# A second score product over 64 rows instead of 128, in an encoder layer with two attention head groups

## The chip, the cores and the metric

The kernel runs on one core of a Trainium2 chip. A core has a matrix engine (TensorE, "PE" in the profile, with its weight loads shown apart as "PEld"), three engines for elementwise work (VectorE "DVE", ScalarE "ACT", GpSimd "POOL"), and queues that issue DMA transfers; nearly all DMAs of this kernel are issued by SyncE ("SP"). The metric is the time in microseconds of one execution on the device, from outside; the profiled execution also has a span, from its first to its last instruction.

## What is computed

One layer on a sequence of 1024 rows of width 1024, in float32. An input projection feeds two groups of eight heads of width 64: attention with a forget gate (FoX, causal) and attention over a band of chunks with a relative-position bias. Both go through an output projection; a cross-attention into 256 memory rows and an MLP of width 4096 follow, each with a norm before and after it. Cut to the part that the change touches:

```python
logits = jnp.einsum('bqhd,bkhd->bhqk', qb, kb).astype(jnp.float32) * scale      # FoX, blocks of 128 queries
logits = logits + c[:, :, q0:q1, None] - c[:, :, None, :q1]
...
logits = jnp.einsum('bcqhd,bckhd->bhcqk', qc, kband).astype(jnp.float32) * scale  # chunked
logits = logits + bias[None, :, None]
...
p = jax.nn.softmax(logits, axis=-1).astype(v.dtype)
out = jnp.einsum('bhcqk,bckhd->bcqhd', p, vband)
```

## The kernel before

**Precision.** TensorE multiplies in a rounded format (`F32R`). To keep float32 accuracy, each operand is split into a hi part (rounded) and a lo part (the remainder), and a product is made of three: hi x hi, hi x lo and lo x hi (`mm3`, lines 191 to 195). A head is only 64 wide, while the array has 128 rows, and the scores use this. For head `a` of a pair, `HALVES[a]` (line 360) names its own 64 rows and the other 64. The tile `qs` holds the queries' hi part in the head's own rows and their lo part in the other rows (lines 837 to 844). The tile `kd` holds the keys' hi part twice, once in each half; the second time by a DMA from SBUF to SBUF. The tile `kl` holds the keys' lo part twice, in the same way. So the first product over 128 rows (line 638) gives q_hi k_hi + q_lo k_hi, and the second one (line 639), accumulated into the same bank of PSUM, gives q_hi k_lo + q_lo k_lo.

**Where the keys come from.** `project_steps` (line 792) makes the projections of a pair of heads. For keys, per half `th` of the 1024 rows and per head `a`: ScalarE copies the hi part into the head's own rows of `kd` (line 847), VectorE subtracts to get the lo part into the own rows of `kl` (line 848), and `copy` (line 849) sends each to the other 64 rows, 128 KB a transfer. Over 8 pairs, 2 halves and 2 heads that makes 32 transfers of `kd` and 32 of `kl`.

**What sets the order.** In the attention phase the order of instructions on every engine is written out while the kernel is built, by a planner (`Flow`, line 56). It keeps an estimated clock for each engine. Steps of TensorE come from generators (`value_steps`, `turn_steps`, `score_steps`, `side_steps`, then the projections as filler), each with a cost and a condition; work for the other engines is put into waiting lists with a due time, a cost and a priority. A DMA costs 0.55 us of the queue there, and lands after the time given. A block of keys and queries counts as ready (`seen["qk", n]`) when twelve parts have reported; `score_steps` (line 604) yields one step per score piece, of up to 512 columns, when its keys, its bias and a bank are there. So what is told to the planner decides in which order score pieces, transposes, value products and projections interleave.

**The score pieces.** A head has eight blocks of 128 queries and twelve pieces. Each piece is the two products at lines 638 and 639, then VectorE adds the bias and takes the minimum (the queries are negated; line 642), ScalarE exponentiates, GpSimd scales. Transposes (line 711) and the products with the values (line 754) follow.

**The start.** While the first loads are under way, TensorE does 17 transposes of the identity (line 1628) into a bank that nobody reads. The first real products are those of the values (lines 1681 and 193 to 195). The squares of the input for its norm (`square`, line 1633) use a ring of two buffers with the tag `phl`, which the attention phase uses later for the split probabilities.

Of the kernel before, what the change touches and what calls it, by code (L numbers as in the profile page):

```python
# [15 lines left out]
F32R = mybir.dt.float32r  # L16
# [6 lines left out]
P = 128  # L23
# [4 lines left out]
HT = 512  # L28
# [6 lines left out]
def f(ap):  # L35
    return ap.bitcast(F32)
# [99 lines left out]
def build(ctx, tc, nc, out, t):  # L136
    def pool(name, bufs=1, space=None, stack=ctx, **kw):
        if space is not None:
            kw["space"] = space
        return stack.enter_context(tc.tile_pool(name=name, bufs=bufs, reuse_waits="tile", **kw))  # L140
# [9 lines left out]
    def mm_tile(shape, name, tag="mm"):  # L150
        return psp.tile(shape, F32, tag=tag, bufs=2, name=name)
# [104 lines left out]
    p1 = pool("p1", stack=p1s)  # L256
# [103 lines left out]
    HALVES = [(slice(a * 64, a * 64 + 64), slice(64 - a * 64, 128 - a * 64)) for a in range(2)]  # L360
    flow = Flow()
# [8 lines left out]
    def mark(key):  # L370
        return lambda at: seen.__setitem__(key, at)
# [179 lines left out]
    bias, qs, kd, kl, vs2, probs, trs, pvs = {}, {}, {}, {}, {}, {}, {}, {}  # L551
# [40 lines left out]
    def block_range(kind, i):  # L592
        return 0 if kind == "f" else max(0, i - 4)
# [10 lines left out]
    def score_steps():  # L604
# [5 lines left out]
        for n, a in heads:  # L610
            kind, pr = ORDER[n]
            h = pr * 2 + a
            for g in groups(n):
                probs[n, a, g] = {}
                for q in (1, 0) if kind == "f" else (0, 1):
                    i = 2 * g + q
                    nm = f"{kind}{h}g{g}{i}"
                    b0 = block_range(kind, i)
                    nk = (i + 1 - b0) * P
                    k0, boff = b0 * P, 0 if kind == "f" else 640 - nk  # L620
                    first = nk if nk <= 512 else 512 if nk - 512 >= 256 else nk - 256
                    pieces = [(0, first), (first, nk - first)] if nk > first else [(0, nk)]
                    mn = small.tile([P, 2], F32, tag="mn", bufs=6, name=f"mn{nm}")
                    fresh = g > 1 or not probs[n, a, g]
                    for j, (o, w) in enumerate(pieces):
                        wide = w
                        last = j == len(pieces) - 1
                        yield (2 * (wide / 2400 + 0.0135),
                               lambda: there(("qk", n), ("bias", n, a)) and free["s"].ready()
                               and (not fresh or j or free["sp"].ready()))  # L630
                        free["s"].take()
                        if fresh and not j:
                            free["sp"].take()
                            tile_ = p1.tile([P, S], F32, tag="sp", bufs=5, name=f"sp{nm}")
                        sp = tile_ if g > 1 else tile_[:, q * HT:(q + 1) * HT]
                        ps = mm_tile([P, HT], f"s{nm}{j}", "s")
                        qb = qs[n, a][:, i * P:(i + 1) * P]
                        nc.tensor.matmul(ps[:, :wide], qb, kd[n, a][:, k0 + o:k0 + o + wide], start=True, stop=False)
                        nc.tensor.matmul(ps[:, :wide], qb, kl[n, a][:, k0 + o:k0 + o + wide], start=False, stop=True)

                        def reduce(o=o, w=w, j=j, ps=ps, sp=sp, mn=mn, bt=bias[n, a], boff=boff):
                            nc.vector.tensor_tensor_reduce(
                                out=sp[:, o:o + w], in0=ps[:, :w], in1=bt[:, boff + o:boff + o + w],
                                scale=1.0, scalar=3e38 if j == 0 else mn[:, 0:1],
                                op0=ALU.add, op1=ALU.min, accum_out=mn[:, j:j + 1])

                        if not last:
                            flow.put("V", flow.end, 0.15 + w / 950, reduce, free["s"].give)
                        else:
                            sm = small.tile([P, 2], F32, tag="sm", bufs=6, name=f"sm{nm}")  # L650
                            exp = lambda sp=sp[:, :nk], m=mn[:, j:j + 1], sm=sm: nc.scalar.activation(
                                sp, sp, AF.Exp, scale=-1.0, bias=m, accum_out=sm[:, 0:1])
                            inv = lambda sm=sm: nc.vector.reciprocal(sm[:, 1:2], sm[:, 0:1])
                            mul = lambda sp=sp[:, :nk], sm=sm: nc.gpsimd.tensor_scalar(
                                sp, sp, sm[:, 1:2], 1.0, op0=ALU.mult, op1=ALU.mult)
                            rest = [("S", 0.25 + nk / 1090, exp), ("V", 0.17, inv), ("G", 0.25 + nk / 1150, mul)]
                            end_of_head = i == (0 if kind == "f" else TB - 1)

                            def after(at, rest=rest, key=("p", n, a, g, q), end_of_head=end_of_head, kind=kind, i=i):
                                free["s"].give(at)  # L660
                                if kind == "f" and i:
                                    mask_block(*key[1:3], i - 1, at)
                                if end_of_head:
                                    free["bias"].give(at)
                                flow.chain(at, rest, mark(key), 0)

                            go = lambda at, w=w, reduce=reduce, after=after: flow.put("V", at, 0.15 + w / 950, reduce, after)
                            if kind == "f":
                                ready[n, a, i] = go
                                masked[n, a, i](flow.end)  # L670
                            else:
                                go(flow.end)
                            probs[n, a, g][q] = sp, b0, i
# [118 lines left out]
    def project_steps(what, n, part):  # L792
# [7 lines left out]
        for th in range(2):  # L800
            cs = slice(th * HT, (th + 1) * HT)
            for kc in range(KC):
                yield (0.681, lambda: kc or there((what, n)) and free["mm"].ready() and
                       (th or free["u4"].ready(u) and (what != "k" or free["klo"].ready(2))))
                if kc == 0:
# [7 lines left out]
                    ps = mm_tile([P, HT], f"{what}{n}_{th}")  # L813
# [17 lines left out]
            for a, (own, oth) in enumerate(HALVES):  # L831
                def last(at, both=both):
                    both.append(at)
                    if len(both) == 2:
                        free["mm"].give(at)

                if what == "q":
                    pv = ps.rearrange("p (a b) -> p a b", b=P)[:, :, ::1 if kind == "f" else -1]
                    dst = qs[n, a].rearrange("p (a b) -> p a b", b=P)[:, th * 4:th * 4 + 4, :]
                    hi = lambda dst=dst, pv=pv, own=own: nc.scalar.activation(dst[own], pv[own], AF.Copy, scale=-0.125)  # L840
                    lo = lambda dst=dst, pv=pv, own=own, oth=oth: nc.vector.scalar_tensor_tensor(
                        dst[oth], pv[own], -0.125, f(dst[own]), op0=ALU.mult, op1=ALU.subtract)
                    flow.put("S", flow.end, 0.6, hi, lambda at, lo=lo, last=last: flow.put(
                        "V", at, 0.7, lo, lambda end: (last(end), part(end)), 1), 1)
                else:
                    d, l = kd[n, a], kl[n, a]
                    hi = lambda d=d, ps=ps, own=own, cs=cs: nc.scalar.activation(d[own, cs], ps[own], AF.Copy)
                    lo = lambda d=d, l=l, ps=ps, own=own, cs=cs: nc.vector.tensor_sub(l[own, cs], ps[own], f(d[own, cs]))
                    copy = lambda x, own=own, oth=oth, cs=cs: nc.sync.dma_start(f(x[oth, cs]), f(x[own, cs]))

                    def then(at, lo=lo, last=last, copy=copy, d=d, l=l):
                        flow.load(at, lambda: copy(d), part, 2.3)
                        flow.put("V", at, 0.7, lo, lambda end: (last(end), flow.load(
                            end, lambda: copy(l), part, 2.3)), 1)

                    flow.put("S", flow.end, 0.6, hi, then, 1)
        free["w"].give(flow.end)
# [751 lines left out]
    with tc.manual_schedule():  # L1609
# [14 lines left out]
        raw0 = [value_raw(0, 0)]  # L1624
        vs = {g: value_tiles(g) for g in (1, 0)}
        warm = mm_tile([P, 4, P], "warm", "tr")
        for n in range(17):
            nc.tensor.transpose(warm[:, n % 4, :], ident, ident)

        sqs = [p1.tile([P, 2, HT], F32, tag="phl", bufs=2, name=f"sqx{j}") for j in range(2)]  # L1630
        sq = [sqs[0][:, 0]]
# [63 lines left out]
        ps = mm_tile([P, 4], "ssx", "pv")  # L1695
# [26 lines left out]
        for th in (1, 0):  # L1722
            tr = mm_tile([P, 4, P], f"rr{th}", "pv")
# [60 lines left out]
    o = [outs[1, h] for h in range(4)]  # L1784
# [206 lines left out]
    for b in range(4):  # L1991
        c = slice(b * P, (b + 1) * P)
        ps = mm_tile([P, HT], f"ym11{b}", "tr" if b < 2 else "pv")
# [36 lines left out]
    k0, k1 = slice(0, HT), slice(HT, D)  # L2030
# [141 lines left out]
    with manual:  # L2172
        sums = lambda: None
        for j in range(NP):
# [10 lines left out]
            if j < AHEAD:  # L2185
                p1, g11 = saved.pop(j)
# [210 lines left out]
        last = inverse_last(7)  # L2397
# [69 lines left out]
```

## Time and profile before

| what | us |
|---|---|
| median of two runs | 1461.92 (1461.62 and 1462.22) |
| span of the profiled execution | 1459.5 |
| VectorE busy in it | 996.0 |
| ScalarE busy in it | 820.7 |
| GpSimd busy in it | 421.0 |
| scores on TensorE, first and last product | about 87 to 472 |

The profile comes from one execution. An engine's busy time is the time covered by its instructions. Matmuls overlap, as they are pipelined, and their ends are modelled; the time that one of them takes of TensorE is better read from the distance between starts. A row of the timeline has the start, the duration, the engine, the line, the operation, the tiles (out, then in) and the shape; in brackets stands the idle time before it and what ended it. Rows in a row with the same line and tile are merged (x8, for instance). In the shape of a matmul, 128*128 is the active rows and columns of the array.

### The profile page before, as it was taken

How to read it: one execution, taken by the hardware profiler on the slowest of the kernel's cores; microseconds unless marked ns; L12 is line 12 of the kernel's file. 1: busy time of each engine (PE TensorE's matmuls, PEld its weight loads, DVE VectorE, ACT ScalarE, POOL GpSimd, SP SyncE). 2: the span in 40 equal slices, each digit the busy share in tenths (PEclk: the TensorE clock that was granted, in tenths of full speed). 3: DMA queues.
4: the chain of work that ended last, by engine and by line, in shares of the span. 5: the costliest groups of instructions: out<-in, count | busy, mean ns of one | idle time of the engine just before them, and what ended most of it. 6: DMA issues, size and time to landing. Idle time of an engine off the chain costs nothing.

```text
span 1459.5 us, 21037 instructions
## 1 busy us (share of the span) xinstructions
PE 1447.7 (99%) x7265; PEld 1222.2 (84%) x7265; DVE 996.0 (68%) x1704; ACT 820.7 (56%) x1437; POOL 421.0 (29%) x520
## 2 busy tenths in 40 slices
PE   9999999999999999999999999999999999999998
PEld 8988888888889888888788888888888888888886
DVE  6777777767668847976873687765555666655576
ACT  6567677766677836555653465545555543444442
POOL 1245456555455301521332414343322000000021
PEclk9999999999999999999999999999999999999999
DMA  7132324321325584552541637754444785445565
GB/s 276 49 95 72 83 67 140 86 82 46 95 58 161 174 314 173 187 179 86 181 138 44 200 132 260 258 196 159 159 151 161 286 318 185 140 149 190 186 246 202
DMA packets 88987, 232.17 MB, mean 159 GB/s; under 512 B 10649, under 2 KB 14753, under 8 KB 88881
## 3 DMA queue, kind: packets, MB, share of 16 engines
q1 hardware_dynamic: 88736, 230.57, 47.6%
q8 instruction: 57, 0.93, 0.3%
q14 instruction: 50, 0.40, 0.1%
q10 hardware_dynamic: 144, 0.26, 0.1%
HBM read 167.30 MB, written 55.11 MB: 152 GB/s over the span
## 4 chain that ended last, share of the span: by engine, by line
PE 96%; DVE 2%; DMA 1%; ACT 1%; issue 0%; SPq 0%; DVEq 0%; ACTq 0%
PE pv L754 4%; PE fx L194 4%; PE fx L193 4%; PE fx L195 4%; PE ptr L711 4%; PE px L194 3%; PE fy L193 3%; PE px L195 3%; PE fy L195 3%; PE px L193 3%; PE fy L194 3%; PE mq L195 2%; PE q L193 2%; PE q L195 2%; PE q L194 2%; PE yw L193 2%
## 5 line engine op out<-in xcount | busy, mean ns | idle before, releaser
L717 DVE TENSOR_TENSOR phl<-ptr,phl 128x512 fp32r<-128x512 f32 (+1 forms) x152 | 92.5, 616 | 31.5 <-ACT phl L720 30.5
L2163 ACT ACTIVATE whif<-ra 128x1024 fp32r<-128x1024 f32 x37 | 39.2, 1061 | 130.3 <-PE fy L194 62.6
L2165 DVE TENSOR_TENSOR wlof<-ra,whif 128x1024 fp32r<-128x1024 f32 x37 | 45.3, 1225 | 91.7 <-ACT whif L2163 91.7
L720 ACT ACTIVATE phl<-ptr 128x512 fp32r<-128x512 f32 (+1 forms) x152 | 79.8, 540 | 40.3 <-PE ptr L711 38.5
L2285 POOL TENSOR_SCALAR rf<-sf 128x1 f32<-128x1 f32 x7 | 7.9, 1130 | 321.7 <-ACT jf L2266 321.4
L754 PE MATMUL pv<-phl,vs 128*128 128x512 f32 (+1 forms) x304 | 85.2, 366 | 0.2 <-DVE phl L717 0.2
L193 PE MATMUL fx<-vhif,whif 128*128 128x512 f32 x168 | 65.4, 389 | 0.0
L195 PE MATMUL fx<-vhif,wlof 128*128 128x512 f32 x168 | 65.4, 389 | 0.0
L194 PE MATMUL fx<-vlof,whif 128*128 128x512 f32 x168 | 65.4, 389 | 0.0
L754 PEld LDWEIGHTS pv<-phl,vs 128*128 128x128 f32 x304 | 55.2, 188 | 11.0 <-DVE phl L717 0.7
L2050 POOL TENSOR_TENSOR sc<-wf,wf 128x512 f32<-128x512 f32 x14 | 23.1, 1652 | 141.1 <-DMA wf<-in_w_ff 122.6
L768 POOL TENSOR_TENSOR o<-o 64x256 f32<-64x256 f32 x64 | 47.8, 747 | 53.1 <-DVE o L766 29.0
L193 PE MATMUL k<-hT_hi,whik 128*128 128x512 f32 x128 | 53.6, 419 | 0.0
L766 DVE TENSOR_TENSOR o<-pv,o 64x512 f32<-64x512 f32 x64 | 44.0, 688 | 13.5 <-ACT o L771 12.1
L193 PE MATMUL q<-hT_hi,whiq 128*128 128x512 f32 x128 | 51.6, 403 | 0.0
L193 PE MATMUL mq<-h2T_hi,whimq 128*128 128x512 f32 x128 | 51.4, 401 | 0.0
L195 PE MATMUL mq<-h2T_hi,wlomq 128*128 128x512 f32 x128 | 50.2, 392 | 0.2 <-DVE wlomq L455 0.2
L195 PE MATMUL k<-hT_hi,wlok 128*128 128x512 f32 x128 | 50.3, 393 | 0.0
L194 PE MATMUL k<-hT_lo,whik 128*128 128x512 f32 x128 | 50.3, 393 | 0.0
L195 PE MATMUL q<-hT_hi,wloq 128*128 128x512 f32 x128 | 50.2, 392 | 0.0
L194 PE MATMUL q<-hT_lo,whiq 128*128 128x512 f32 x128 | 50.2, 392 | 0.0
L194 PE MATMUL mq<-h2T_lo,whimq 128*128 128x512 f32 x128 | 50.1, 392 | 0.1
(696 smaller groups left out, 5014.5 us busy)
## 6 DMA issues: line engine op xcount, KB each, us to landing
ra<-gd SPq DMA_DIRECT2D x56, 512.0 KB, 3.8
wg<-in_w_ff SPq DMA_DIRECT2D x56, 512.0 KB, 5.6
wf<-in_w_ff SPq DMA_DIRECT2D x38, 512.0 KB, 3.9
gd<-s SPq DMA_DIRECT2D x48, 256.0 KB, 2.1
wrawmq<-in_w_mq SPq DMA_DIRECT2D x16, 512.0 KB, 4.3
gd<-u SPq DMA_DIRECT2D x32, 256.0 KB, 2.2
gd<-g SPq DMA_DIRECT2D x25, 256.0 KB, 2.2
wrawq<-in_w_qk SPq DMA_DIRECT2D x8, 512.0 KB, 4.4
```

What stands on the lines that cost most here:

```text
L193: nc.tensor.matmul(ps, lh, rh, start=start, stop=False, skip_group_check=more)
L194: nc.tensor.matmul(ps, lh, rl, start=False, stop=False, skip_group_check=more)
L195: nc.tensor.matmul(ps, ll, rh, start=False, stop=stop, skip_group_check=more)
L711: nc.tensor.transpose(tr[:, m, :], sp[:, k * P:(k + 1) * P], ident)
L717: flow.put("V", at, 0.7, lambda: nc.vector.tensor_sub(pl[:, live, :], tr[:, live, :], f(ph[:, live, :])), done)
L720: flow.put("S", flow.end, 0.6, lambda ph=ph, tr=tr, live=live: nc.scalar.activation(ph[:, live, :], tr[:, live, :], AF.Copy), split)
L754: nc.tensor.matmul(pv[:, :, qs_, :], v, hl[:, :, hs, :], start=c == 0 and turn == 0, stop=last)
L766: flow.put("V", at, 0.7, lambda: nc.vector.tensor_add(o2[own], pv[own, :, :, ::step], o2[own]), lambda end: (free["pv"].give(end), flow.pu ...
L768: free["pv"].give(end), flow.put("G", end, 0.8, lambda: nc.gpsimd.tensor_add(o2[own, 0], o2[own, 0], o2[own, 1]), store)))
L2050: eng.tensor_sub(sc[:, k1], r0[:, k0], r1[:, k0])
L2163: nc.scalar.activation(ah, ra, AF.Copy)
L2165: nc.vector.tensor_sub(al, ra, f(ah))
```

## The change

Three edits. The second product of a score piece takes the head's own 64 rows of `qs` and `kl` alone, so that it gives q_hi k_lo, without q_lo k_lo. The other half of `kl` is then read by nobody, and its copy goes: VectorE's subtraction reports the part as ready itself, where the landing of the copy did. In the warm-up, 4 transposes stay, and 12 products of 512 columns follow on a tile of ones (`unit`, in the ring `phl`, filled by VectorE): over the lower 64 rows, the upper 64 rows or all 128. Products over the upper rows go to a second bank.

```diff
                         nc.tensor.matmul(ps[:, :wide], qb, kd[n, a][:, k0 + o:k0 + o + wide], start=True, stop=False)
-                        nc.tensor.matmul(ps[:, :wide], qb, kl[n, a][:, k0 + o:k0 + o + wide], start=False, stop=True)
+                        own = HALVES[a][0]
+                        nc.tensor.matmul(ps[:, :wide], qb[own], kl[n, a][own, k0 + o:k0 + o + wide], start=False, stop=True)
...
                         flow.load(at, lambda: copy(d), part, 2.3)
-                        flow.put("V", at, 0.7, lo, lambda end: (last(end), flow.load(
-                            end, lambda: copy(l), part, 2.3)), 1)
+                        flow.put("V", at, 0.7, lo, lambda end: (last(end), part(end)), 1)
...
         warm = mm_tile([P, 4, P], "warm", "tr")
-        for n in range(17):
+        other = mm_tile([P, 4, P], "warm2", "tr")
+        unit = p1.tile([P, HT], F32R, tag="phl", bufs=2, name="unit")
+        nc.vector.memset(f(unit), 1.0)
+        lowr, highr = slice(0, 64), slice(64, P)
+        for n in range(4):
             nc.tensor.transpose(warm[:, n % 4, :], ident, ident)
+        for part in (lowr, highr, lowr, highr, lowr, highr, slice(0, P), lowr, slice(0, P), lowr, lowr, slice(0, P)):
+            nc.tensor.matmul((other if part is highr else warm).rearrange("p a b -> p (a b)"), unit[part, :P], unit[part, :],
+                             start=True, stop=True)
```

In the built program each 64-row product is marked as a tile of 64 x 128 at row 0 or 64 of the array, and all others but eight as 128 x 128. Those eight, the transposes of the forget gates (line 521), are marked 128 x 32.

## The prediction

> **What bounds the kernel now.** I read the page first: the span, TensorE's busy time and clock, and the chain of work that ended last.
>
> ```profile
> span 1459.5 us, 21037 instructions
> PE 1447.7 (99%) x7265; PEld 1222.2 (84%) x7265; DVE 996.0 (68%) x1704; ACT 820.7 (56%) x1437; POOL 421.0 (29%) x520
> ...
> PEclk9999999999999999999999999999999999999999
> ...
> PE 96%; DVE 2%; DMA 1%; ACT 1%; issue 0%; SPq 0%; DVEq 0%; ACTq 0%
> ```
>
> TensorE (PE) is busy for 99% of the span at its full granted clock, and 96% of the chain runs through it. So an edit pays here only if it takes time away from TensorE, and any time it adds to TensorE is paid in full. Next comes the stretch in which the scores are computed, in the view by windows (columns: length, then busy time of PE, PEld, DVE, ACT and POOL, granted clock, DMA share, GB/s).
>
> ```profile
> 84.00:475.00 391.00, 390.42 (x2175) 333.86 (x2175) 285.28 (x774) 275.53 (x560) 204.15 (x303) 1.00 0.32 89
> ```
>
> In 391 us TensorE is not busy for 0.58 us; no earlier operand can win more than that there. The DMA engines are busy for 0.32 of the stretch. Third, the waits of TensorE:
>
> ```profile
> PE warm L1628 <- POOL ident masks.py:199: 1.3, 1, 1.3
> PE v L193 <- ACT hT_hi L1648: 0.9, 1, 0.9
> PE v L194 <- DVE wlov L319: 0.6, 1, 0.6
> ...
> PE sc3g L638 <- DVE mnc3g L642: 0.3, 1, 0.3
> ```
>
> The longest are at the very start. Among the scores, TensorE waits for VectorE's reduction, never for the keys' lo parts or their copies.
>
> **The copies that go.** Each of the 32 half-blocks of keys loses one DMA from kl to kl.
>
> ```profile
> kl<-kl SPq DMA_DIRECT2D x32, 128.0 KB, 2.4
> ```
>
> ```profile
> L849 SPq DMA_DIRECT2D kl<-kl x32: 461/465/1240, 76.2 to 449.5; - x32
> ```
>
> SyncE saves 32 x 0.465 = 14.9 us of issuing, and each block's keys count as ready up to 2.4 us sooner. The copy of the hi part (kd), which every first product needs, stays and is issued earlier in the chain than the lo part is made, so the readiness of a block of keys now ends with that copy or with VectorE's subtraction. What was queued on SyncE behind a kl copy (kd copies, weight loads, bias loads, stores of attention output) moves up. In the built program the planner, which is told of 2.35 us less, also brings the first score pieces of a block one projection step forward and deals the later ones out differently. None of this is on TensorE's path beyond the 0.58 us above. I take 0, with bounds of -0.6 us (all idle time gone) and +1 us (a new order that meets as many stalls again as the old one has). If the cover were gone, that is, if TensorE were idle and waiting for the keys, the gain would be one landing of 2.4 us per block of keys.
>
> **The second product over 64 rows.** Its count and widths, from the view of line 639 (one chunked and one forgetting head):
>
> ```profile
> L639 PE MATMUL sc0g<-kl,qs x12: 276/309/393, 87.1 to 95.6; 128*128 128x256 f32 x5, 128*128 128x384 f32 x5, 128*128 128x128 f32 x1, 128*128 128x512 f32 x1
> ...
> L639 PE MATMUL sf0g<-kl,qs x12: 274/338/397, 168.2 to 188.1; 128*128 128x512 f32 x5, 128*128 128x384 f32 x3, 128*128 128x256 f32 x3, 128*128 128x128 f32 x1
> ```
>
> Twelve products a head over 16 heads are 192. They move 5 x 256 + 5 x 384 + 128 + 512 = 3840 columns in a chunked head and 4608 in a forgetting head, 8 of each, so 67,584 in all. What a product costs is seen from start to start, since the recorded durations overlap. Here is TensorE around the first scores, and then its weight loads:
>
> ```profile
> 88.18 0.44 PE L638 MATMUL sc0g<-kd,qs 128*128 128x384 f32 x1
> 88.46 0.34 PE L639 MATMUL sc0g<-kl,qs 128*128 128x384 f32 x1
> ...
> 89.78 0.33 PE L638 MATMUL sc0g<-kd,qs 128*128 128x384 f32 x1
> 89.95 0.34 PE L639 MATMUL sc0g<-kl,qs 128*128 128x384 f32 x1
> ```
>
> ```profile
> 88.17 0.19 PEld L638 LDWEIGHTS sc0g<-kd,qs 128*128 128x128 f32 x1 [0.28 <-DVE mnc0g L642]
> ...
> 89.55 0.19 PEld L638 LDWEIGHTS sc0g<-kd,qs 128*128 128x128 f32 x1
> ```
>
> A product of 384 columns takes 0.17 us of the stream (89.78 to 89.95), and one of 512 takes 0.23 (59.34 to 59.57, below): the time goes with the columns that move. The change leaves these as they are and halves only the rows. So the 192 products keep their 67,584 / 384 x 0.17 = 29.9 us, and I take no saving. The bounds on this term are 0 and half of it, -15 us; no row has a product over 64 rows, and nothing shows rows being paid for.
>
> What is new is that TensorE changes between 128 rows and 64. In the built program every one of the 192 products has a 128-row one before and after it: 384 changes. The price of one is not in the trace; two rows stand around it.
>
> From below: for the forget gates, eight transposes with 8 columns of weights (128*8, built as a 128 x 32 tile) stand between products over the whole array, on TensorE and in its weight loads:
>
> ```profile
> 59.34 0.39 PE L195 MATMUL q<-hT_hi,wloq 128*128 128x512 f32 x1
> 59.57 1.03 PE L521 MATMUL ftr<-ident,fcol 128*8 128x128 f32 x8
> 60.36 0.48 PE L193 MATMUL q<-hT_hi,whiq 128*128 128x512 f32 x1
> 60.68 0.40 PE L194 MATMUL q<-hT_lo,whiq 128*128 128x512 f32 x1
> ```
>
> ```profile
> 59.34 0.97 PEld L521 LDWEIGHTS ftr<-ident,fcol 128*8 128x8 f32 x8
> 60.33 0.19 PEld L193 LDWEIGHTS q<-hT_hi,whiq 128*128 128x128 f32 x1
> 60.44 0.19 PEld L194 LDWEIGHTS q<-hT_lo,whiq 128*128 128x128 f32 x1
> ```
>
> ```profile
> L521 PE MATMUL ftr<-ident,fcol x8: 270/272/273, 59.6 to 60.3; 128*8 128x128 f32 x8
> ```
>
> The way in costs 0.23 (59.34 to 59.57), what 512 columns take at the 0.17 of 384. Within the eight the spacing is (1.03 - 0.27) / 7 = 0.11, so the last starts at 60.33. The loads of the q products follow at 60.33 and 60.44, the same 0.11 apart, and the second q product starts 0.24 after that, its usual 0.23 and a hundredth. Nothing is left for the two changes: 0.00 to 0.01 us each. But these change columns of the array, not the rows in which data and weights enter.
>
> From above: at 88.17 TensorE had waited, so that the load of the weights ran with no product over it. From that product to the next were 0.28 us, against 0.17 for the same 384 columns at 89.78, whose load had begun at 89.55 under the product before. A load without cover costs 0.11. If TensorE had moreover to see the product before to its recorded end (0.39 against 0.23 in the stream), that adds 0.16, and a change costs 0.27.
>
> I take the middle, **0.11 us a change: the load loses its cover**. At present each load enters all 128 rows while a product streams through the same 128 rows; with another set of rows in use before than after, this overlap is what I expect to go. It is a choice between 0.00 and 0.27, nearer to the 88.17 row because rows are what the change alters. 384 x 0.11 = **42.2 us**, with bounds of 0 and 384 x 0.27 = 104 us.
>
> The page "TensorEngine Tiling (Array Packing)" of the Trainium skill, Key Properties, says that a change of tiling mode drains TensorE, while a change of tile does not. By it each change would cost the 0.16 us tail, 384 x 0.16 = 61 us; the forget gates' transposes, a change from 128 x 128 to 128 x 32, show no such drain, and no run here shows a change of rows.
>
> **The warm-up.** A memset on VectorE and twelve products of 512 columns stand in for 13 transposes.
>
> ```profile
> 1.34 3.51 PE L1628 MATMUL warm<-ident 128*128 128x128 f32 x17 [1.34 <-POOL ident masks.py:199]
> ...
> 4.08 0.69 DVE L319 TENSOR_TENSOR wlov<-wrawv,whiv 128x512 fp32r<-128x512 f32 x1 [3.17 <-POOL whiv L316]
> ...
> 5.07 0.71 PE L1681 MATMUL v<-whiv,hT_hi 128*128 128x256 f32 x4 [0.22 <-ACT hT_hi L1648]
> ...
> 9.55 0.36 PE L193 MATMUL v<-whiv,hT_hi 128*128 128x256 f32 x1 [0.87 <-ACT hT_hi L1648]
> ```
>
> The memset falls into 3.17 us in which VectorE is idle. The transposes start 0.2 apart here ((3.51 - 0.27) / 16, the last one taken at 0.27 as above), about twice the 0.11 of those at 59.57. Four of them end at about 2.1; twelve products at 0.23 to 0.46 (that same doubling) then last until 4.9 to 7.6. The first real product would start up to 2.5 us late, of which the 0.87 us of waiting before 9.55 absorb a part, and the 0.6 us wait for wlov more. I take 0, at most +1 us. The new tile also takes a buffer in the ring of the squares; the second square needs it, about 10 us into the span, and the warm-up is over by then.
>
> **The sum.** 0 + 0 + 42.2 + 0. The profiled execution has a span of 1459.5 us, 2.4 under the median of 1461.92, which I carry as it is: 1461.9 + 42.2 = **1504.1 us**.
>
> **The rivals.** About 2%, 29 us, is what a measurement of this kernel can tell from no change; over 384 changes that is 0.076 us each.
> - *Each change is free.* For it: the 0.00 to 0.01 at the forget gates. Against: those were no changes of rows. TensorE then has the same stream, and the time is 1461.9, less 0.6 or plus 2 at most: **1462**, not slower. Chance 0.28.
> - *Only the way back costs.* The load of 64 rows goes ahead as before, and only that of 128 rows, half of which enter rows just used apart, is uncovered: 192 x 0.11 = 21 us, **1483**, within 2% still. For and against: nothing in the trace parts the two directions. Chance 0.14.
> - *Each change empties the array*, and the tail is paid: 384 x 0.16 = 61 us, **1523**; with an uncovered load 0.27 and 1566. For it: the recorded durations outlast the spacing by 0.16, so there is something to empty. Against: the forget gates again. The skill's rule above is this rival. Chance 0.23, of it 0.06 above 1545.
> - *Halves run beside other work*: if the 192 products hid wholly under their neighbours, 29.9 us would go: **1432**. Against: each neighbour uses all 128 rows. Half of the saving is already within 2%. Chance 0.03.
> - The forecast, 0.076 to 0.14 us a change, 1491 to 1516: chance 0.32.
>
> **How the numbers follow.** Faster by over 2%: 0.03. Within 2%: 0.28 + 0.14 = 0.42. Slower by over 2%: 0.32 + 0.23 = 0.55. The range takes in the free case with its bounds below, and the emptying case up to 0.21 us a change: 1459 to 1543. Left out are halves side by side, the emptying with an uncovered load, and the edges, some 0.12 together. The forecast's own range is 1491 to 1516.
>
> **What would show it.** From an L639 product to what follows, start to start, 0.28 instead of 0.17 at 384 columns, and as much before it; weight loads of L640 (new number) that start with the end of the product before, not with its start; the score stretch longer by about 42 us with no new row among the waits, for this is inside TensorE; everything after the scores equal. The same spacing as now proves the free case; 0.33 to 0.44 the emptying one. The warm-up's alternation of both halves will show by its spacing whether halves run side by side. The forecast is wrong, too, if the new order of the scores adds waits of whole microseconds for VectorE or ScalarE.

## The result and the profile after

| what | before | after |
|---|---|---|
| median, us | 1461.92 (1461.62 to 1462.22) | 1532.41 (1532.13 to 1532.69) |
| ratio to before, 95% interval | | 1.0485 [1.0454, 1.0515] |
| span of the profiled execution, us | 1459.5 | 1530.3 |

The changed kernel is 70.5 us slower. Its page, in the lines that were shown of before:

```profile
span 1530.3 us, 20964 instructions
## 1 busy us (share of the span) xinstructions
PE 1520.6 (99%) x7264; PEld 1229.0 (80%) x7264; DVE 1002.0 (65%) x1705; ACT 821.2 (54%) x1437; POOL 416.9 (27%) x520
...
PEclk9999999999999999999999999999999999999999
...
PE 98%; DVE 1%; issue 0%; ACT 0%; DVEq 0%; POOL 0%; POOLq 0%; ACTq 0%
```

TensorE is busy for 73 us more (1520.6 against 1447.7) with one matmul fewer, at the same clock. The chain of work that ended last runs through it even more than before (98% against 96%). So the time is inside TensorE. Where in the span? Two places bound it, each in the view of one line of the changed kernel: the forget gates' transposes just ahead of the scores, and the sums of squares (line 1059) just behind them.

```profile
L521 PE MATMUL ftr<-ident,fcol x8: 271/272/273, 59.7 to 60.4; 128*8 128x128 f32 x8
```

```profile
L1059 PE MATMUL ssh<-o,sq x32: 164/250/250, 579.6 to 652.5; 128*128 128x1 f32 x32
```

And the second one before the change:

```profile
L1059 PE MATMUL ssh<-o,sq x32: 164/250/250, 509.0 to 581.9; 128*128 128x1 f32 x32
```

Ahead of the scores the two kernels are 0.1 us apart (59.57 before, in the prediction), behind them 70.6 us (579.6 - 509.0), and 70.8 us at the end of the spans (1530.3 - 1459.5): nearly all of it came between. The scores last longer than the table ahead of the prediction says: their last product starts at 485.0 before and at 554.3 after the change. So the view by windows, with the columns as in the prediction, stops some ten microseconds short of their end in both kernels:

```profile
84.00:545.00 461.00, 461.00 (x2207) 342.48 (x2206) 291.68 (x781) 277.98 (x563) 206.57 (x305) 1.00 0.24 68
```

TensorE counts as busy for all of it, but its weight loads cover 342 of 461 us, where they covered 334 of 391: the gaps are in the loads. The waits of TensorE show nothing new on the score products:

```profile
PE warm L1632 <- POOL ident masks.py:199: 1.3, 1, 1.3
PE pv L755 <- DVE phl L718: 0.9, 1, 0.9
PE ym L193 <- ACT junk L1073: 0.4, 1, 0.4
PE mq L195 <- DVE wlomq L455: 0.2, 1, 0.2
```

One wait is longer than before: at 555.2, just behind the last score product, TensorE waits 0.9 us for the split probabilities (0.2 before). From 556.3 on it then has half its clock for 3.4 us, which can cost up to 1.7 us (granted clock 0.57 in these four microseconds):

```profile
556.00:560.00 4.00, 3.89 (x12) 3.13 (x13) 3.48 (x10) 2.02 (x4) 2.33 (x3) 0.57 0.85 284
```

These two are a part of the 70.6 us. The rest is among the scores, and the timeline shows where, early among them: first the products, then the weight loads.

```profile
86.67 0.39 PE L195 MATMUL q<-hT_hi,wloq 128*128 128x512 f32 x1
86.90 0.33 PE L638 MATMUL sc0g<-kd,qs 128*128 128x384 f32 x1
87.16 0.43 PE L640 MATMUL sc0g<-kl,qs 64*128 64x384 f32 x1
87.52 0.50 PE L638 MATMUL sc0g<-kd,qs 128*128 128x512 f32 x1
87.96 0.50 PE L640 MATMUL sc0g<-kl,qs 64*128 64x512 f32 x1
88.38 0.50 PE L193 MATMUL q<-hT_hi,whiq 128*128 128x512 f32 x1
88.72 0.40 PE L194 MATMUL q<-hT_lo,whiq 128*128 128x512 f32 x1
```

```profile
86.67 0.19 PEld L638 LDWEIGHTS sc0g<-kd,qs 128*128 128x128 f32 x1
87.16 0.18 PEld L640 LDWEIGHTS sc0g<-kl,qs 64*128 64x128 f32 x1 [0.30 <-issue]
87.52 0.19 PEld L638 LDWEIGHTS sc0g<-kd,qs 128*128 128x128 f32 x1 [0.18 <-issue]
87.95 0.18 PEld L640 LDWEIGHTS sc0g<-kl,qs 64*128 64x128 f32 x1 [0.25 <-issue]
88.38 0.19 PEld L193 LDWEIGHTS q<-hT_hi,whiq 128*128 128x128 f32 x1 [0.24 <-issue]
88.49 0.19 PEld L194 LDWEIGHTS q<-hT_lo,whiq 128*128 128x128 f32 x1
```

Where the rows stay at 128, a load starts together with the product before it (86.67). Where they change, the load starts only together with its own product (87.16, 87.52, 87.95, 88.38), after an idle time that no semaphore ends ("issue"). At 88.38 both parts of the price can be read. The load takes 0.11 us (88.38 to 88.49, when the next load may begin). The product at 87.96 had its own load until 88.06, and its 512 columns take some 0.22 more, until about 88.28; the next load waits until 88.38. So TensorE also stands for about 0.10 us before the load. That it waits there until the product is out of the array ("emptying" from here on) is my inference; a fixed time for the change itself would look the same.

### The profile page after: what moved, and what is told of

The parts are those of the page before. It is cut to its first block, busy times and chain, and to the rows that moved or that the text cites. A ratio compares the mean times of both kernels' runs of the same rounds, so it can differ in the third digit from the quotient of the medians.

```text
span 1530.3 us, 20964 instructions
## 1 busy us (share of the span) xinstructions
PE 1520.6 (99%) x7264; PEld 1229.0 (80%) x7264; DVE 1002.0 (65%) x1705; ACT 821.2 (54%) x1437; POOL 416.9 (27%) x520
## 4 chain that ended last, share of the span: by engine, by line
PE 98%; DVE 1%; issue 0%; ACT 0%; DVEq 0%; POOL 0%; POOLq 0%; ACTq 0%
PE pv L755 4%; PE ptr L712 4%; PE fx L194 4%; PE fx L195 4%; PE fx L193 4%; PE px L195 3%; PE px L193 3%; PE fy L194 3%; PE fy L195 3%; PE px L194 3%; PE fy L193 3%; PE q L193 2%; PE k L193 2%; PE v L193 2%; PE mq L195 2%; PE k L195 2%
## 5 line engine op out<-in xcount | busy, mean ns | idle before, releaser
L755 PE MATMUL pv<-phl,vs 128*128 128x512 f32 (+1 forms) x304 | 88.5, 376 | 0.9 <-DVE phl L718 0.9
L193 PE MATMUL q<-hT_hi,whiq 128*128 128x512 f32 x128 | 55.9, 437 | 0.0
L772 ACT ACTIVATE o<-pv 64x512 f32<-64x512 f32 x64 | 37.8, 592 | 33.3 <-issue 12.6
```

The costliest lines, as they stand in the source:

```text
L193: nc.tensor.matmul(ps, lh, rh, start=start, stop=False, skip_group_check=more)
L755: nc.tensor.matmul(pv[:, :, qs_, :], v, hl[:, :, hs, :], start=c == 0 and turn == 0, stop=last)
L772: flow.put("S", flow.end, 0.6, lambda: nc.scalar.activation(o2[own], pv[oth, :, :, ::step], AF.Copy), both)
```

## The experiments

**The rows alone, and the copies alone.** The first run takes the 64-row product into the kernel before, and leaves copies, due times and warm-up. The second leaves the product at 128 rows, drops the copies, and has GpSimd zero the half of `kl` that they filled, which leaves out q_lo k_lo as the change does.

```diff
+++ rows alone
-  nc.tensor.matmul(ps[:, :wide], qb, kl[n, a][:, k0 + o:k0 + o + wide], start=False, stop=True)
+  nc.tensor.matmul(ps[:, :wide], qb[HALVES[a][0]], kl[n, a][HALVES[a][0], k0 + o:k0 + o + wide], start=False, stop=True)
+++ copies alone
   kl[n, a] = p1.tile([P, S], F32R, tag="klo", bufs=4, name=f"kl{n}{a}")
+  nc.gpsimd.memset(f(kl[n, a][HALVES[a][1]]), 0.0)
...
-  flow.put("V", at, 0.7, lo, lambda end: (last(end), flow.load(
-      end, lambda: copy(l), part, 2.3)), 1)
+  flow.put("V", at, 0.7, lo, lambda end: (last(end), part(end)), 1)
```

> The second product over 64 rows alone; the kl copies, the planner's due times and the warm-up stay as before, so the order of all engines is that of before. Theory (each of 384 changes between 128 and 64 rows empties TensorE and leaves a weight load uncovered, 0.184 us each by the changed kernel's 70.5 us): 1462 + 70 = 1532 us. Rival 1 (the planner's new order without the copies brings the stalls): 1462. A mixture would lie between, and the rest would be in the run without copies.

Measured: 1530.85 us against 1461.62 beside it, ratio 1.0472 [1.0454, 1.0489]. The edit alone carries the loss: 69.2 us, 0.180 us for each of 384 changes. No wait of its own lies among the scores, and its clock stays at 1.00 up to the mark behind them (line 1059), so this is the cleanest price. The planner's order is that of before, so rival 1 falls.

> No kl copies, as in the change, but the second product stays over 128 rows; GpSimd sets the other half of kl to zero, so that the product is q_hi k_lo alone, as in the changed kernel. Theory: 1462, within 1 us either way, since TensorE is idle for 0.58 us of the score stretch and no row changes. Rival 1 (the new order costs): towards 1532. Rival 2 (a gain from the 32 copies gone that the row changes hid): below 1460.

Measured: 1464.59 us, ratio 1.0018 [1.0009, 1.0028]: 3 us slower, outside the 1 us of the theory, and no gain from the 32 copies, so rival 2 falls. The profile names the stall, one wait of 2.2 us for the split probabilities (the same line of the view says 0.2 in the kernel before), and behind it, as in the changed kernel, 3.4 us at half the clock:

```profile
PE pv L754 <- DVE phl L717: 2.2, 1, 2.2
```

```profile
488.00:492.00 4.00, 3.56 (x10) 2.89 (x11) 3.53 (x10) 2.02 (x4) 2.48 (x4) 0.57 0.86 284
```

So dropping the copies gives nothing, and this version of it brings a small stall of its own. Whether the zeroing on GpSimd or the new order makes that stall was not tried; the changed kernel, without the zeroing, waits 0.9 us for the same tiles at the same place, behind the last score product.

**The warm-up alone.** The diff is the last part of the change.

> The changed warm-up alone. Theory: 1462.0 to 1462.5; the forget gates' transposes stand 0.09 us later in the changed kernel's trace (59.66 against 59.57), although the first real product is 2.8 us late. Rival: a late start that costs its 2.8 us, 1464.7.

Measured: 1462.83 us, ratio 1.0008 [0.9998, 1.0017]: a little above the expected range, but the interval holds no difference. A start that costs 2.8 us would be 1.0019, outside the interval.

**Fewer changes with as many 64-row products.** A block of queries with more than 512 keys has two pieces. Here both 128-row products come first, then both 64-row ones, which leaves 256 changes. The same step with 128-row products is the control; it is made from the kernel before, so that it also keeps the copies and the old warm-up.

```diff
-  for j, (o, w) in enumerate(pieces):
-      yield (2 * (wide / 2400 + 0.0135),
...
+  yield (2 * (wides / 2400 + 0.0135 * len(pieces)),
+         lambda: there(("qk", n), ("bias", n, a)) and free["s"].ready(len(pieces))
...
+  for ps, (o, wide) in zip(banks, pieces):
+      nc.tensor.matmul(ps[:, :wide], qb, kd[n, a][:, k0 + o:k0 + o + wide], start=True, stop=False)
+  for ps, (o, wide) in zip(banks, pieces):
+      nc.tensor.matmul(ps[:, :wide], qb[own], kl[n, a][own, k0 + o:k0 + o + wide], start=False, stop=True)
```

> The changed kernel with the score pieces of one block of queries in one step: where a block has two pieces, first both 128-row products, then both 64-row ones. As many 64-row products (192), but 256 changes of rows instead of 384. Theory (price per change): 1532.4 - 128 x 0.184 = 1509, plus what the coarser step costs the planner's order (the same grouping with 128 rows shows that). Rival 3 (each 64-row product is dear by itself, whatever stands before it): 1532.

> The kernel before with the same grouping of pieces, second product over 128 rows and copies kept: the control for the grouping. Theory: 1462 to 1464, as TensorE's work is the same and only the step is coarser. If the grouping itself costs more, that is to be taken off the grouped 64-row kernel's time.

Measured: 1515.71 us (ratio 1.0371 [1.0355, 1.0386]) over 64 rows, and 1468.57 (1.0053 [1.0036, 1.0070]) in the control, which is more than expected. The control's waits on VectorE at line 639, the first product of the coarser step, are new or longer than before; they look like waits for banks.

```profile
PE sc0g L639 <- DVE mnc0g L647: 1.6, 3, 1.2
...
PE yw L193 <- ACT yw L1203: 1.3, 1, 1.3
PE sc2g L639 <- DVE mnc2g L647: 0.9, 2, 0.7
```

Between the two lie 47.1 us for 256 changes: 0.184 us each, as 70.5 / 384 in the changed kernel. That the two agree to the last digit is luck. The grouped kernel and its control differ in copies and warm-up as well, and the grouped kernel has two stretches of 3.4 us at half the clock (from 198.0 and from 559.8), which its control has not; without these, worth up to 3.4 us, it would be 0.171 us. So the price here is 0.17 to 0.18 us. The number of 64-row products is that of the changed kernel (192), so rival 3, by which the loss would have stayed at 70 us, falls: the price is that of the change. In the weight loads of the grouped kernel two 64-row loads (the "x2") share one wait:

```profile
90.59 0.29 PEld L641 LDWEIGHTS sc0g<-kl,qs 64*128 64x128 f32 x2 [0.19 <-issue]
91.07 0.19 PEld L193 LDWEIGHTS q<-hT_hi,whiq 128*128 128x128 f32 x1 [0.19 <-issue]
```

**Another number of rows, the same tiling.** Head 0 of each pair takes its second product over 96 rows.

```diff
+  rs = slice(0, 96) if a == 0 else slice(0, P)
-  nc.tensor.matmul(ps[:, :wide], qb, kl[n, a][:, k0 + o:k0 + o + wide], start=False, stop=True)
+  nc.tensor.matmul(ps[:, :wide], qb[rs], kl[n, a][rs, k0 + o:k0 + o + wide], start=False, stop=True)
```

> Second product over rows 0 to 95 for head 0 of each pair (half of its q_lo k_lo terms left out), 128 for head 1; all else as before. In the built program a product over 96 rows is a 128 x 128 tile, so the tiling does not change although the number of active rows does, 192 times. Theory (the price is that of another tiling of the array): 1462. Rival 4 (any other set of rows uncovers the load): 192 x 0.184 = 35 us more, 1497.

Measured: 1462.01 us against 1461.38, ratio 1.0004 [0.9995, 1.0014]. The timeline has 96 active rows, and the spacing of before:

```profile
90.18 0.33 PE L638 MATMUL sc0g<-kd,qs 128*128 128x384 f32 x1
90.35 0.34 PE L640 MATMUL sc0g<-kl,qs 96*128 96x384 f32 x1
90.52 0.39 PE L193 MATMUL q<-hT_hi,whiq 128*128 128x512 f32 x1
```

0.17 us for 384 columns. Rival 4 falls: another number of active rows costs nothing by itself. What the 64-row product has beside it is the tile of the array that it is marked with, 64 x 128 against 128 x 128; that this mark decides is what remains, for 64 rows were not run under the other mark.

**The price by itself.** 128 products on a tile of ones stand in for the warm-up transposes.

```diff
+  def probe(bank, rows, cols=P, wide=HT):
+      nc.tensor.matmul(banks[bank][:cols, :wide], unit[rows, :cols], unit[rows, :wide], start=True, stop=True)
...
+  for _ in range(8):
+      probe(1, full), probe(0, lowr)
```

> Products on a tile of ones in place of the warm-up, read from the spacing of their starts at the full clock, 512 columns unless said; total some 50 us over 1462. Theory: 128 rows after 128: 0.23 us. 64 after 64: 0.23, or 0.41 by rival 3 (64 rows dear by themselves). 128 and 64 in turn: 0.41. The same with 128 columns: 0.25 (0.107 of load, 0.05 of columns, 0.09 to empty). Lower and upper 64 rows in turn, two banks: two products per 0.23. 128 and 96 rows in turn: 0.23, or 0.41 by rival 4. 128 columns of weights and 32 in turn: 0.23 if the columns' tiling is free, as at the forget gates; 0.41 if those eight transposes were an exception. 64 and 32 rows in turn: 0.41.

Measured in one execution, 1498.29 us, 37 more than before; the spacings, worked out from the starts in its trace:

```
in turn                                   us from start to start
128 rows, 128 rows       512 columns      0.22 to 0.24
64, 64 (the same half)   512              0.22 to 0.24
128, 64                  512              0.42 to 0.43
128, 64                  128              0.25 to 0.26 (the first five); 0.40 at half clock
lower 64, upper 64       512              0.43 for two at half clock, 0.23 for the last two at full clock
128, 96                  512              0.23 to 0.24
128 columns of weights, 32                0.23
64, 32 rows              512              0.42 to 0.43; 0.72 at half clock
```

The spacings came as expected, but for the clock (below); the total came out lower than the "some 50 us" over 1462. A change costs 0.43 - 0.23 = 0.20 us between products of 512 columns. Between those of 128 it costs 0.25 - 0.11 = 0.14, since there the spacing without a change is that of the loads, 0.11. The scores have widths of 128 to 512, and their 0.17 to 0.18 lies between. The half clock tells something of the emptying. In the changed kernel's 3.4 us at half clock, transposes start 0.21 us apart, which is their loads (0.11 at full clock), and products of 512 columns 0.43 apart (558.10 to 558.52). That leaves 0.72 - 0.21 - 0.43 = 0.08 us of a change for the emptying, against 0.43 - 0.11 - 0.23 = 0.09 at full clock. So this part, by estimate, does not stretch with the granted clock as loads and columns do. The probe's weight loads show the same break as the kernel, with nothing else on the engine:

```profile
9.07 1.68 PEld L1633 LDWEIGHTS warm<-unit 64*128 64x128 f32 x8 [0.35 <-issue]
11.12 0.19 PEld L1633 LDWEIGHTS warm<-unit 128*128 128x128 f32 x1 [0.36 <-issue]
11.55 0.18 PEld L1633 LDWEIGHTS warm<-unit 64*128 64x128 f32 x1 [0.24 <-issue]
11.97 0.19 PEld L1633 LDWEIGHTS warm<-unit 128*128 128x128 f32 x1 [0.24 <-issue]
```

Eight loads of 64 rows in a row follow one another without a gap that the view marks, hence one merged line; from the first change on, each load stands alone after 0.24 to 0.36 us of idle time.

## Why the prediction was right, and what was too small

- *The bound.* Right: TensorE is the bound, and what it loses is paid (70.5 us of time, 70.6 between the two marks). But "not busy for 0.58 us" was no measure of what it could gain, since a busy TensorE can stand still between a product and a load, as the changed kernel shows.
- *The copies at 0.* Right in that they bring no gain; the run without them, with GpSimd's zeroing, is 3 us slower, where +1 was the bound.
- *The 64-row product keeps its time.* Right: 64 after 64 rows takes the 0.23 us of 128 after 128.
- *The warm-up at 0.* Right: 1.0008 [0.9998, 1.0017]. The first real product starts 2.8 us late (7.88 against 5.07; up to 2.5 was forecast), and by the forget gates' transposes all but 0.1 is absorbed.
- *"0.11 us a change: the load loses its cover".* One part of the mechanism, of two. That the load loses its cover is shown, by the loads that start with their own product; that the loss goes with the changes is shown by their counts (0.17 to 0.18 us each at 256 and at 384). The term was too small: 42.2 us against 70.5, and the forecast's own range, 1491 to 1516, was missed. The load is 0.11 of the price. The rest is the stand before it, which I had given to a rival as an alternative; it comes in addition. Its price there, 0.16, was too high, for it was taken from the recorded ends, which are modelled; the loads put it at about 0.10.
- *The range.* That 1459 to 1543 held the result is in part luck: by the forecast's own mechanism it would have ended at 1516, and it reached further only to take in the rival of the emptying.
- *The signs.* The spacing from a 64-row product of 384 columns to the next is 0.36 (87.16 to 87.52): not the 0.28 of the forecast, but within the 0.33 to 0.44 that was to prove the emptying. The other signs held: late weight loads, and the same work after the scores in the same time, within 0.2 us.
- *The rivals.* Free changes (1462), a price on the way back only (1483) and halves beside their neighbours (1432) are out: both directions cost, as the loads at 87.16 and 87.52 show. The emptying rival came nearest. Alone (1523) it lacks the uncovered load; with the load (1566, in the part with a chance of 0.06) it is right in kind and too dear by its 0.16. The rule of the page "TensorEngine Tiling (Array Packing)" of the Trainium skill, Key Properties, that a change of tiling mode drains TensorE, agrees for rows with what is measured, the stand of about 0.10 us before each late load. For columns it doesn't: 128 x 128 and 128 x 32 in turn take 0.23 us, the spacing without a change, as the forget gates' transposes had shown.

## What to carry to other kernels

Count the changes between 128-row and 64-row products, not the rows saved (64 and 32 rows in turn cost as much in the probe): at full clock each cost 0.17 to 0.20 us here (0.14 between products of 128 columns), close to a whole product of 512 columns, because TensorE stands still and then loads weights with nothing over them. If a half of the rows has nothing to add, fill it, with a copy or with zeros, or take 96 rows (from row 0; run for half of the heads), which stayed in the 128-row tiling. If 64 rows are wanted, put such products in long runs; the grouped kernel shows the gain from runs of two, and longer ones, or the two halves side by side, were run in the probe alone. On a bound engine, look at the idle time of its weight loads, for the busy share of its products (99% in both kernels) hides such stalls.

## What the runs showed of the hardware beside that

Products over the lower and the upper half of the rows, in two banks, run side by side: the last two in the probe, at full clock, take 0.23 us, as long as one over 128 rows, and two of them at half clock take 0.43, as long as one over 128 rows in the changed kernel's stretch at half clock.

Changes of rows may also cost clock. In the probe the granted clock fell to half twice, though TensorE counts as busy throughout: at 19.2, while 128-row and 64-row products of 128 columns took turns, and at 39.7, while 64-row and 32-row products of 512 columns did. The view by windows of the probe, columns: length, then PE, PEld, DVE, ACT and POOL, clock, DMA share, GB/s:

```profile
12.00:18.00 6.00, 6.00 (x16) 2.61 (x15) 0.00 (x0) 0.00 (x0) 0.68 (x2) 1.00 1.03 396
19.00:23.00 4.00, 4.00 (x12) 2.87 (x11) 0.00 (x0) 0.00 (x0) 0.00 (x0) 0.52 0.46 183
28.00:34.00 6.00, 6.00 (x28) 4.24 (x26) 0.00 (x0) 0.00 (x0) 0.00 (x0) 1.00 0.00 0
40.00:42.00 2.00, 2.00 (x4) 0.78 (x3) 0.00 (x0) 0.00 (x0) 0.00 (x0) 0.50 0.00 0
```

The first row has changes at 512 columns, the third has none of rows. Narrow products are not needed for it, since the second fall came at 512 columns. Nor does a fall answer at once: the first came 8 us after the changes had begun (at 11.1), the second 5.4 us after the turns with 32 rows had (at 34.3). That the many short stalls read as too little activity is my guess; no run shows it. Among the changed kernel's scores the clock stayed at 1.00.

In three kernels 3.4 us at half clock began within 2 us of a wait of 0.9 to 2.2 us (the changed one, the one without copies and the grouped one). Behind waits of 1.2 and 1.3 us in the grouped control, and one of 1.6 us in the grouped kernel, there was no such fall. What decides there stays open too.
